# Narrow row loads on GpSimd's own queue, in seven widths, with loads leading stores by six batches

## Chip, cores, metric

One core of one Trainium2 chip. The metric is device time in microseconds of the whole program, median of repeated runs. Ratios below are the mean time of one kernel's fast runs over that of the other's of the same rounds, so not quite the ratio of the medians quoted.

## The reference

A softmax over rows of 256 floats of which only the first `length` count; the rest of the output is zero. There are 16 batches of 2048 rows and one length for a batch, drawn between 128 and 255.

```python
for b in range(batch):
    length = lengths[b]
    masked = x[b, :, :, :length].copy()
    masked = masked - np.max(masked, axis=-1, keepdims=True)
    exp_masked = np.exp(masked)
    result[b, :, :, :length] = exp_masked / np.sum(exp_masked, axis=-1, keepdims=True)
```

The draw is fixed; the prediction lists it. A row is 1024 bytes; columns past the length need not be read.

## The kernel before

A batch sits in SBUF, the core's on-chip memory, as 128 partitions of 16 rows (16 KB to a partition), in one of 12 slots. VectorE clips the columns past the length to a huge negative number, ScalarE takes exponentials and row sums, VectorE scales by the reciprocal sums, and SyncE stores the batch whole. All loads and stores of x go through SyncE's queue, the list of transfers issued by SyncE that the core's 16 DMA engines work off. For each batch SyncE reads the length and loads 160 (or 168), 208 or all 256 columns:

```python
    slots = min(12, batch)
    behind = 2
    widths = [[160, 208], [168, 208]]
    # ...
        def part(b, h, w):
            s = slice(h * half, (h + 1) * half)
            nc.sync.dma_start(
                out=xt[:, b % slots, s, :w], in_=x_f[b, :, s, :w]
            ).then_inc(s_ld[b], 16)
    # ... narrow(b, w): both halves by part; whole(b): one transfer of 2.1 MB
        def load(b):
            pick(length(SP, b), widths[b % 2], lambda w: narrow(b, w), lambda: whole(b))
    # ... batch 0: first half whole, second half by length
        for b in range(1, slots):
            nc.sync.wait_ge(s_fill, b + 1)
            load(b)
        for b in range(batch):
            nc.sync.wait_ge(s_out, b + 1)
            nc.sync.dma_start(out=out_f[b], in_=xt[:, b % slots]).then_inc(s_st[b], 16)
            n = b + slots - behind
            if b >= behind and n >= slots and n < batch:
                nc.sync.wait_ge(s_st[n - slots], 16)
                load(n)
    # ... GpSimd zeroes columns 160 to 255 of all 12 slots first (s_fill; of slot 0 only the second half)
```

A load of whole partitions is one run of 16 KB for each partition; a narrow load is 2048 runs of 640 to 832 bytes, since the columns that are skipped lie between them.

The softmax here doesn't subtract the row's maximum and nothing guards it: scores larger than these inputs give would overflow.

## Time and profile before

| | before |
|---|---|
| time | 162.62 us (162.17 to 162.66, 4 runs) |
| span of the profile | 161.5 us |
| SyncE's queue, share of 16 engines' span | 98.7% |
| VectorE, ScalarE, GpSimd busy | 131.6, 105.2, 15.9 us |
| read and written | 30.28 and 33.55 MB |

The row to look at is the third: the DMA engines are busy all the time and the compute engines are not. "Share" counts the time of packets in flight over 16 engines. The lines are in the prediction.

### The profile page before, as it was taken

To read this page: it belongs to the slowest core of one execution; us is meant where nothing else is said; L and a number is where in the kernel's file an instruction comes from. 1 tells how busy PE (TensorE), PEld (TensorE's weight loads), DVE (VectorE), ACT (ScalarE), POOL (GpSimd) and SP (SyncE) were. 2 spreads that over 40 slices of the span, in tenths; PEclk is the share of its full clock that TensorE was granted. 3 is DMA by queue.
4 is the path that set the end of the run, shared out by engine and by line. 5 is a ranking of instruction groups with operands and counts; after the bars stand their busy time and mean duration, and the time that the engine had idled before them with its cause. 6 is when DMAs were issued, how large, how long until landed. Compare 5 with 4: busy or idle time off the path is not lost.

```text
span 161.5 us, 1141 instructions
## 1 busy us (share of the span) xinstructions
PE 0.2 (0%) x1; PEld 0.1 (0%) x1; DVE 131.6 (82%) x99; ACT 105.2 (65%) x514; POOL 15.9 (10%) x18
## 2 busy tenths in 40 slices
PE   0000000000000000000000000000000000000000
PEld 0000000000000000000000000000000000000000
DVE  4999878999999999999999999999999999000000
ACT  3000089999989797987979797978979892000000
POOL 8999100000000000000000000000000000000000
DMA  5999999999999999999999999999999999999980
GB/s 134 406 414 442 422 378 406 390 356 449 418 376 403 392 290 436 426 430 387 408 405 392 437 430 410 434 422 432 434 422 438 430 430 434 434 426 434 430 357 20
DMA packets 17269, 63.86 MB, mean 396 GB/s; under 512 B 626, under 2 KB 13938, under 8 KB 13938
## 3 DMA queue, kind: packets, MB, share of 16 engines
q1 hardware_dynamic: 17264, 63.83, 98.7%
q14 instruction: 3, 0.02, 0.0%
q10 hardware_dynamic: 2, 0.00, 0.0%
HBM read 30.28 MB, written 33.55 MB: 395 GB/s over the span
## 4 chain that ended last, share of the span: by engine, by line
DVE 65%; issue 15%; ACT 3%; DVEq 1%; POOL 1%; ACTq 0%; PE 0%; POOLq 0%; SPq 0%
DVE xt L206 29%; DVE xt L179 21%; DVE iota_h L154 9%; DVE cap L164 3%; ACT xt L222 3%; DVE inv_sum L204 2%; DVEq L192 1%; POOL xt L132 0%; ACTq L222 0%; POOL iota_i L134 0%; DVEq L191 0%; DVEq L82 0%; DVE len_s L158 0%; PE len_f L143 0%; POOL ones L133 0%
## 5 line engine op out<-in xcount | busy, mean ns | idle before, releaser
L222 ACT ACTIVATE xt<-xt x256 | 102.4, 403 | 27.6 <-DVE xt L179 27.6
L206 DVE TENSOR_TENSOR xt<-xt,inv_sum 128x2048 f32<-128x2048 f32 x32 | 73.4, 2292 | 1.1
L222 ACT ACTIVATION_READ_ACCUMULATOR xt<-xt x256 | 48.3, 188 | 0.0
L179 DVE TENSOR_TENSOR xt<-xt,cap 128x2048 f32<-128x2048 f32 x16 | 36.5, 2283 | 0.3 <-DVE cap L164 0.3
L154 DVE TENSOR_SCALAR iota_h<-iota_i 128x256 f32<-128x256 int32 x1 | 14.6, 14629 | 2.2 <-POOL iota_i L134 2.2
L138 POOL MEMSET xt<- 128x1536 f32 x11 | 14.6, 1367 | 0.0
L204 DVE RECIPROCAL inv_sum<-row_sum 128x8 f32<-128x8 f32 x32 | 6.3, 195 | 1.7 <-ACT xt L222 1.7
L164 DVE TENSOR_SCALAR cap<-iota_h,len_s 128x256 f32<-128x256 f32 x16 | 5.5, 346 | 0.0
L215 ACT ACT_TABLE_LOAD x1 | 1.3, 1283 | 1.5 <-SPq L63 1.5
L132 POOL MEMSET xt<- 128x768 f32 x1 | 0.7, 737 | 0.5 <-SPq L63 0.5
L158 DVE COPY len_s<-len_f 128x16 f32<-128x16 f32 x1 | 0.2, 173 | 0.3 <-PE len_f L143 0.3
L134 POOL IOTA iota_i<- 128x256 int32 x1 | 0.3, 331 | 0.0
L215 ACT ACTIVATE warm<-const-float32-0.0 128x1 f32<-128x1 f32 x1 | 0.2, 203 | 0.0
L133 POOL MEMSET ones<- 1x128 bf16 x1 | 0.2, 194 | 0.0
L143 PE MATMUL len_f<-len_b,ones 1*128 1x16 bf16 x1 | 0.2, 164 | 17.1 <-DVE len_b L156 17.1
L156 DVE CAST len_b<-word 1x16 bf16<-1x16 int32 x1 | 0.1, 150 | 0.0
L244 POOL MEMSET const-float32-0.0<- 128x1 f32 x1 | 0.1, 98 | 0.2 <-issue 0.2
L143 PEld LDWEIGHTS len_f<-len_b,ones 1*128 1x128 bf16 x1 | 0.1, 99 | 17.0 <-issue 17.0
L244 POOL MEMSET const-bfloat16-1.0<- 128x1 bf16 x1 | 0.1, 101 | 0.0
L244 POOL MEMSET const-uint8-127<- 128x1 uint8 x1 | 0.1, 101 | 0.0
L244 POOL MEMSET const-float32-1.0<- 128x1 f32 x1 | 0.1, 98 | 0.0
## 6 DMA issues: line engine op xcount, KB each, us to landing
out_dram<-xt SPq DMA_DIRECT2D x16, 2048.0 KB, 24.0
xt<-in_x_dram SPq DMA_DIRECT2D x9, 2048.0 KB
xt<-in_x_dram SPq DMA_DIRECT2D x9, 832.0 KB, 13.2
xt<-in_x_dram SPq DMA_DIRECT2D x2, 672.0 KB, 12.3
xt<-in_x_dram SPq DMA_DIRECT2D x2, 640.0 KB, 11.6
xt<-in_x_dram SPq DMA_DIRECT2D x1, 1024.0 KB, 5.2
word<-in_lengths_dram ACTq DMA_DIRECT2D x1, 0.1 KB
```

Source lines behind the costliest of these rows:

```text
L132: nc.gpsimd.memset(xt[:, 0, half:, low:], 0.0).then_inc(s_fill, 1)
L138: nc.gpsimd.memset(xt[:, b, :, low:], 0.0).then_inc(s_fill, 1)
L143: nc.tensor.matmul(len_f, lhsT=ones, rhs=len_b, start=True, stop=True).then_inc(s_lenf, 1)
L154: step(nc.vector.tensor_scalar(out=iota_h, in0=iota_i, scalar1=0.5, scalar2=None, op0=ALU.add))
L164: nc.vector.tensor_scalar(out=cap[:, b % 4, :], in0=iota_h, scalar1=len_s[:, b : b + 1], scalar2=-1.0e30, op0=ALU.subtract, op1=ALU.mult,)
L179: return nc.vector.tensor_tensor(out=t[:, :, lo:hi], in0=t[:, :, lo:hi], in1=cap[:, b % 4, None, lo:hi].to_broadcast([P, nt, hi - lo]), op ...
L192: with nc.vector.If(v_len < mid):
L204: step(nc.vector.reciprocal(out=inv_sum[:, b, s], in_=row_sum[:, b, s]))
L206: ins = nc.vector.tensor_tensor(out=t[:, s, :], in0=t[:, s, :], in1=inv_sum[:, b, s, None].to_broadcast([P, half, seq_k]), op=ALU.mult,)
L215: nc.scalar.activation(out=warm, in_=nc.const_aps.tensor(0.0, (P, 1), F32), func=EXP)
L222: ins = nc.scalar.activation(out=e, in_=e, func=EXP, accum_out=row_sum[:, bass.ds(i, 1), j],)
L244: nc = _bacc.Bacc("TRN2", target_bir_lowering=False, num_devices=1)
```

## The change

Three things at once. Narrow loads leave SyncE's queue for GpSimd's own; GpSimd, which is nearly idle, can afford a tree of branches over seven widths. SyncE keeps whole loads and stores. And SyncE's loads lead its stores by six batches, where twelve batches were loaded first and later loads led by ten; the first six are now loaded whole before the lengths are known. GpSimd's loads do not follow the stores: those of batches 6, 9 and 11 are issued as soon as the memsets are done.

```diff
-    behind = 2
-    widths = [[160, 208], [168, 208]]
-    low = 160
+    ahead = min(6, batch)
+    widths = [160, 168, 176, 184, 192, 200, 208]
+    low = widths[0]
@@ one transfer for a batch, on the engine given
+        def narrow(engine, b, w):
+            engine.dma_start(
+                out=xt[:, b % slots, :, :w], in_=x_f[b, :, :, :w]
             ).then_inc(s_ld[b], 16)
+        def pick(v, b, ws):
+            if len(ws) == 1:
+                if ws[0] < seq_k:
+                    narrow(nc.gpsimd, b, ws[0])
                 return
+            m = (len(ws) - 1) // 2
+            with nc.gpsimd.If(v <= ws[m]):
+                pick(v, b, ws[: m + 1])
+            with nc.gpsimd.Else():
+                pick(v, b, ws[m + 1 :])
+        narrow(nc.sync, 0, seq_k)
         nc.scalar.dma_start(out=word64, in_=lengths[None, :]).then_inc(s_word, 16)
+        for b in range(1, ahead):
+            narrow(nc.sync, b, seq_k)
@@ in SyncE's loop, after the store of b
+            n = b + ahead
+            if n < batch:
+                if n < slots:
+                    nc.sync.wait_ge(s_fill, n - ahead + 1)
+                else:
+                    nc.sync.wait_ge(s_st[n - slots], 16)
+                v = length(SP, n)
+                with nc.sync.If(v > widths[-1]):
+                    narrow(nc.sync, n, seq_k)
@@ GpSimd: memsets for slots 6 to 11 only, then its own loads
+        nc.gpsimd.wait_ge(s_word, 16)
+        for n in range(ahead, batch):
+            if n < slots:
+                nc.gpsimd.wait_ge(s_fill, n - ahead + 1)
+            else:
+                nc.gpsimd.wait_ge(s_st[n - slots], 16)
+            v = length(POOL, n)
+            pick(v, n, widths + [seq_k])
@@ VectorE
-            nc.vector.wait_ge(s_ld[b], 32)
+            nc.vector.wait_ge(s_ld[b], 16)
```

More of the change, by code (lines that the diff above doesn't have):

```diff
@@ L17 @@
 ACT = mybir.EngineType.Activation
+POOL = mybir.EngineType.Pool
 @with_exitstack
@@ L86, in length @@
             )
-        def part(b, h, w):
-            s = slice(h * half, (h + 1) * half)
-            nc.sync.dma_start(
-                out=xt[:, b % slots, s, :w], in_=x_f[b, :, s, :w]
+        def narrow(engine, b, w):
+            engine.dma_start(
+                out=xt[:, b % slots, :, :w], in_=x_f[b, :, :, :w]
             ).then_inc(s_ld[b], 16)
-        def narrow(b, w):
-            for h in range(2):
-                part(b, h, w)
-        def whole(b):
-            nc.sync.dma_start(out=xt[:, b % slots], in_=x_f[b]).then_inc(s_ld[b], 32)
-        def pick(v, ws, short, full):
-            if not ws:
-                full()
-                return
-            with nc.sync.If(v <= ws[0]):
-                short(ws[0])
-            with nc.sync.Else():
-                pick(v, ws[1:], short, full)
-        def load(b):
-            pick(length(SP, b), widths[b % 2], lambda w: narrow(b, w), lambda: whole(b))
-        part(0, 0, seq_k)
+        def pick(v, b, ws):
+            if len(ws) == 1:
+                if ws[0] < seq_k:
+                    narrow(nc.gpsimd, b, ws[0])
+                return
+            m = (len(ws) - 1) // 2
[4 more added lines that the diff above has]
+        narrow(nc.sync, 0, seq_k)
         nc.scalar.dma_start(out=word64, in_=lengths[None, :]).then_inc(s_word, 16)
+        for b in range(1, ahead):
+            narrow(nc.sync, b, seq_k)
         nc.sync.wait_ge(s_word, 16)
-        nc.sync.wait_ge(s_fill, 1)
-        pick(length(SP, 0), widths[0], lambda w: part(0, 1, w), lambda: part(0, 1, seq_k))
-        for b in range(1, slots):
-            nc.sync.wait_ge(s_fill, b + 1)
-            load(b)
         for b in range(batch):
@@ L124 @@
             nc.sync.dma_start(out=out_f[b], in_=xt[:, b % slots]).then_inc(s_st[b], 16)
-            n = b + slots - behind
-            if b >= behind and n >= slots and n < batch:
-                nc.sync.wait_ge(s_st[n - slots], 16)
-                load(n)
+            n = b + ahead
[7 more added lines that the diff above has]
+                    narrow(nc.sync, n, seq_k)
         nc.sync.wait_ge(s_st[-1], 16 * slots)
-        nc.gpsimd.memset(xt[:, 0, half:, low:], 0.0).then_inc(s_fill, 1)
         nc.gpsimd.memset(ones, 1.0).then_inc(s_ones, 1)
@@ L136 @@
         ).then_inc(s_iota, 1)
-        for b in range(1, slots):
+        for b in range(ahead, slots):
             nc.gpsimd.memset(xt[:, b, :, low:], 0.0).then_inc(s_fill, 1)
+        nc.gpsimd.wait_ge(s_word, 16)
[6 more added lines that the diff above has]
+            pick(v, n, widths + [seq_k])
         nc.tensor.wait_ge(s_ones, 1)
```

## The prediction

> **What bounds the kernel now.** I read the page's engine and DMA lines first, then the waits of SyncE's queue, then the DMA views of stretches in which only one kind of row moves.
>
> ```profile
> PE 0.2 (0%) x1; PEld 0.1 (0%) x1; DVE 131.6 (82%) x99; ACT 105.2 (65%) x514; POOL 15.9 (10%) x18
> ...
> DMA  5999999999999999999999999999999999999980
> ...
> q1 hardware_dynamic: 17264, 63.83, 98.7%
> ...
> HBM read 30.28 MB, written 33.55 MB: 395 GB/s over the span
> ```
> One DMA queue, SyncE's, keeps the 16 DMA engines busy for 98.7% of the span, from the second slice to the last but one. No compute engine comes near.
>
> ```profile
> SPq L124 <- DVE xt L206: 49.1, 11, 7.0
> SPq L123 <- DMA out_dram<-xt: 22.5, 1, 22.5
> ```
> SyncE's wait for stores at the end lasts 22.5 us, after the last compute: a backlog of stores is drained. The chain of waits names VectorE for 65% of the span, because it follows semaphores and a queue's backlog is not one; I set it aside. VectorE needs about 7.35 us a batch (from one batch's long operations to the next in the chain), against two transfers of nearly 4.9 us for the DMA. So only two things move the end: the work given to the DMA engines, and gaps in which they have none.
>
> Four stretches of the view by windows, the first three with 832-, 672- and 640-byte rows, the last with whole transfers (its last two columns are DMA share and GB/s):
>
> ```profile
> 48.00:51.00 3.00, 0.00 (x0) 0.00 (x0) 2.97 (x3) 3.00 (x17) 0.00 (x0) 1.00 1.13 360
> 57.50:60.50 3.00, 0.00 (x0) 0.00 (x0) 3.00 (x3) 3.00 (x16) 0.00 (x0) 1.00 1.14 287
> 76.60:79.10 2.50, 0.00 (x0) 0.00 (x0) 2.47 (x3) 2.50 (x13) 0.00 (x0) 1.00 1.16 375
> 110.00:140.00 30.00, 0.00 (x0) 0.00 (x0) 27.03 (x22) 22.06 (x110) 0.00 (x0) 1.00 1.01 431
> ...
> DMA packets 1298, 0.86 MB, mean 287 GB/s; under 512 B 16, under 2 KB 1298, under 8 KB 1298
> ...
> DMA packets 1413, 0.94 MB, mean 375 GB/s; under 512 B 21, under 2 KB 1410, under 8 KB 1410
> ```
> In the third, 1410 less 21 completion writes makes 1389 rows in 2.5 us, 356 GB/s; three 16 KB packets raise the 375. The first, in finer slices, stands at 355 until its last. Per row and engine (16 engines x bytes / rate): 640 B cost 28.8 ns, 672 B 37.5, 832 B 37.5. At the whole-row rate (26.9 B/ns an engine) they would cost 23.8, 25.0 and 30.9. The overhead is 5.0, 12.5 and 6.6 ns; 672 is an odd multiple of 32 bytes, the others are even ones. A batch of 2048 rows gives each engine 128, so a load takes 3.68 us (640 B), 4.80 (672 B), 4.80 (832 B), and a whole one, 2.097 MB at 431 GB/s, 4.87. A narrow row saves bytes and almost no time.
>
> **What the Trainium skill says.** "DMA: Bandwidth & Descriptors", section "Why small descriptors are slow (HBM only)", gives a fixed overhead of about 3 cycles a packet, which packing several descriptors into one packet amortizes. The direction agrees; this trace's 5 to 12.5 ns is more. Its section "SWDGE vs HWDGE vs iDMA" says that transfers issued from GpSimd have descriptors made by software, written to rings in SBUF, in packets of preferably at most 4096 B. "Queues, rings and completion order" says that each engine goes round robin over its queues, changing only between packets. With one busy queue the trace shows neither. "SBUF — State Buffer", section "SBUF: two separate sides", says that VectorE's two-port modes and GpSimd exclude each other for a whole instruction. This agrees:
>
> ```profile
> L154 DVE TENSOR_SCALAR iota_h<-iota_i 128x256 f32<-128x256 int32 x1 | 14.6, 14629 | 2.2 <-POOL iota_i L134 2.2
> L138 POOL MEMSET xt<- 128x1536 f32 x11 | 14.6, 1367 | 0.0
> L164 DVE TENSOR_SCALAR cap<-iota_h,len_s 128x256 f32<-128x256 f32 x16 | 5.5, 346 | 0.0
> ```
> A conversion of 256 columns takes 14.6 us, as long as the eleven memsets beside it; operations of that size otherwise take 0.35 us.
>
> **The change part by part.** The lengths are fixed: 188 233 229 243 195 252 165 210 222 180 209 157 159 199 214 248.
>
> Bytes. Before: nine whole loads and the half of batch 0; 832 B for the other half and batches 4, 6, 9, 13; 672 B for batch 11; 640 B for batch 12. After: batches 0 to 5 whole without a test, 7, 8, 10, 14, 15 whole too; batch 6 gets 672 B, 9 gets 736, 11 and 12 get 640, 13 gets 800. That is 30.21 MB against 30.28. The seven widths pay back what the six untested loads give away; bytes gain nothing.
>
> DMA time at the rates above. Before: 16 stores x 4.87 = 77.9; 9.5 whole loads 46.3; 4.5 of 832 B 21.6; one of 672 B 4.8; one of 640 B 3.7; sum 154.3 us. The other 7.2 us of the 161.5 us span are the start, the landing of the last store and small losses. After: stores 77.9; eleven whole loads 53.6; 672 B 4.8; two of 640 B 7.4; 736 and 800 B have no measured row. With 672's overhead (odd multiples of 32 as well) they cost 39.9 and 42.2 ns, 5.1 and 5.4 us; with 6 ns, 4.3 and 4.6. Sum 152.6 to 154.2 us: minus 1.7 to minus 0.1. So with unchanged overheads almost nothing happens.
>
> Packing. If GpSimd's descriptors go six (640, 672 B) or five (736, 800 B) to a packet, most overhead is shared. With 1 to 4 ns left on a row, the five loads have rows of 24.8-27.8 (twice), 26-29, 28.4-31.4 and 30.7-33.7 ns: 128 x 135 to 150 ns = 17.2 to 19.2 us, where the unpacked ones took 21.1 to 22.7. That takes 2 to 5.5 us from the sum.
>
> Start. Five fewer large memsets and none of the half: six x 1.37 = 8.2 us, so the conversion ends near 10 instead of 16.9 and the first mask starts near 11.5 instead of 18.4. The first store can be issued near 23 us (11.5 us from first mask to first result, as before). It gains nothing by itself: six whole loads keep the queue full to 3 + 6 x 4.87 = 32 us, and the narrow loads of 6, 9 and 11 are added from about 12 us.
>
> GpSimd's work: five software transfers and some 50 branches, beside everything. Its descriptor writing may hold up VectorE's 0.35 us operations, perhaps 10 us each time in the worst case; VectorE has 9.7 - 7.35 = 2.4 us of slack a batch and has begun 7 us earlier. Hidden, unless writing takes much longer.
>
> Lead of six. When load n lands, stores and loads of about four batches stand behind it, 39 us, while its own result needs under 15. No gap, provided the narrow load lands in turn.
>
> **The rivals.** (1) Neutral: the overhead of a row belongs to the engine, not the packet. For: the busy share exceeds 1 by only 0.13 in narrow stretches, so rows are handled nearly one after another. Time: 161 to 163 us. (2) Packing: 157 to 160 us. For: what the skill says of GpSimd's packets. Against: no trace of this kernel shows a GpSimd transfer. (3) Starving: each turn passes one row against a 16 KB packet (16384 B at 26.9 B/ns = 0.61 us). Then a narrow load needs 128 x 0.64 = 82 us beside a full queue. Batch 6 then arrives when SyncE's queue runs dry: six loads, stores 0 to 4 and loads 7, 8, 10 are 14 x 4.87 = 68 us, so with some narrow rows between at about 78 us. VectorE masks b+1 before it scales b, so eleven results remain, 11 x 7.35 = 81 us, and a last store of 7 us: 166 to 168 us. With packets of five or six rows a narrow load takes 22 to 26 turns of 0.61 + 0.16 us, about 20 us; batch 6 lands near 40 us, the others follow at 20 us each, all ahead of need. (4) A GpSimd row costs more, since engines must fetch descriptors from SBUF: 5 ns on 640 rows an engine is plus 3.2 us, 165.
>
> **Range and chances.** I hold packing the likeliest, at the weak end of its gain: the overhead is mostly shared, with something lost on switching queues. From 162.6 us, about 3.6 off: 159.0 us. Faster by over 2% (below 159.3): 0.43. Within 2%: 0.34, rival 1 or half of packing. Slower: 0.23, starving or dearer rows. The range is 155 (all overhead gone, VectorE never late) to 168 (starving).
>
> **What would show it.** A stretch with narrow rows beside whole ones moves over 400 GB/s if rows are packed, not 290 to 360. A new software queue carries about 10240 rows, 7.1 MB. The conversion lasts some 8 us instead of 14.6. SyncE's last wait is still long (over 10 us) if the queue never runs dry; if starving, VectorE has an idle gap of ten us or more at batch 6, before 80 us, DMA share falls after it, and that last wait shrinks to one store's time. If VectorE's short operations grow to many us later on, the lock was underrated. I am wrong if a narrow row costs as much on GpSimd's queue as on SyncE's.

## The result

| | before | changed |
|---|---|---|
| time | 162.62 us | 160.40 us (160.11 to 160.63, 4 runs) |
| span of the profile | 161.5 us | 158.5 us |
| SyncE's queue, share | 98.7% | 86.0% |
| GpSimd's queue, share | none | 11.4% |
| read | 30.28 MB | 30.21 MB |

The ratio is 0.9869 (95% interval 0.9843 to 0.9894): 1.3% faster, within 2%. The prediction's figure was 159.0, and the result lies in its range of 155 to 168; but "faster by over 2%" was its likeliest class and did not come. The page of the changed kernel:

```profile
PE 0.2 (0%) x1; PEld 0.1 (0%) x1; DVE 125.6 (79%) x99; ACT 105.1 (66%) x514; POOL 14.5 (9%) x17
...
q1 hardware_dynamic: 3888, 56.62, 86.0%
q0 software_dynamic: 1696, 7.14, 11.4%
...
HBM read 30.21 MB, written 33.55 MB: 402 GB/s over the span
...
L181 DVE TENSOR_TENSOR xt<-xt,cap 128x2048 f32<-128x2048 f32 x16 | 36.6, 2287 | 12.4 <-DMA xt<-in_x_dram 12.0
L91 POOL DMA_DIRECT2D xt<-in_x_dram x5 | 5.9, 1175 | 41.5 <-issue 41.5
L156 DVE TENSOR_SCALAR iota_h<-iota_i 128x256 f32<-128x256 int32 x1 | 8.0, 8030 | 1.6 <-POOL iota_i L128 1.6
```

The queue lines give packets, MB and share. A packet is the piece that an engine moves before it turns to another queue; a completion write is a packet of 4 bytes, 16 to a transfer. GpSimd's queue moved the 10240 rows of its five loads in only 1696 packets, of which 80 are completion writes: a packet holds six or seven rows (4416 to 4800 bytes in the packet records). It took 11.4% of 158.5 us, 18.1 us of every engine for five loads; whole loads would take 24.4. The DMA is nearly as full as before: 97.5% of the span together, against 98.7%. The waits of SyncE's queue:

```profile
SPq L114 <- DVE xt L208: 107.2, 15, 12.3
SPq L113 <- DVE xt L208: 18.6, 1, 18.6
SPq L113 <- DMA out_dram<-xt: 14.3, 1, 14.3
```

The last line says that 14.3 us of stores are still queued when nothing else is left. So the 12.0 us for which VectorE stood waiting for loads cost nothing: the DMA never ran dry.

The gain therefore lies in DMA time, and so does what is missing from it. This is a stretch of the DMA view with batch 6's 672-byte rows on one queue and the whole loads of batches 2 and 3 on the other (no store is issued before 22.7 us, and the first stands behind them):

```profile
DMA packets 468, 4.67 MB, mean 389 GB/s; under 512 B 16, under 2 KB 16, under 8 KB 250
## 3 DMA queue, kind: packets, MB, share of 16 engines
q1 hardware_dynamic: 234, 3.57, 78.2%
q0 software_dynamic: 234, 1.10, 23.0%
```

It covers 12 us. The queues pass packet for packet, 234 to 234. A packet of GpSimd's is 1.10 MB / 234 = 4704 bytes, seven rows. Of SyncE's 234, 16 are completion writes; the 218 of 16 KB took 78.2% of 16 x 12 us, 689 ns each, where 16 KB at the whole-row rate take 610. GpSimd's took 23.0%, 189 ns, where 4704 bytes would take 175. A turn, one packet of each queue, thus carries 79 + 14 = 93 ns too much, 13 ns for each of seven rows. That is what such a row cost on SyncE's queue (12.5 ns in the kernel before). The overhead is not gone, only charged mostly to the packet next to it.

### The profile page after: what moved, and what is told of

It reads as the page before. It is cut to its first block, busy times and chain, and to the rows that moved or that the text cites. A ratio compares the mean times of both kernels' runs of the same rounds, so it can differ in the third digit from the quotient of the medians.

```text
span 158.5 us, 1141 instructions
## 1 busy us (share of the span) xinstructions
PE 0.2 (0%) x1; PEld 0.1 (0%) x1; DVE 125.6 (79%) x99; ACT 105.1 (66%) x514; POOL 14.5 (9%) x17
## 3 DMA queue, kind: packets, MB, share of 16 engines
q0 software_dynamic: 1696, 7.14, 11.4%
HBM read 30.21 MB, written 33.55 MB: 402 GB/s over the span
## 4 chain that ended last, share of the span: by engine, by line
DVE 48%; DMA 26%; issue 11%; ACT 3%; DVEq 0%; SPq 0%; POOL 0%; ACTq 0%; PE 0%; POOLq 0%
DMA xt<-in_x_dram 26%; DVE xt L208 23%; DVE xt L181 15%; DVE iota_h L156 5%; ACT xt L224 3%; DVE cap L166 2%; DVE inv_sum L206 2%; DVEq L194 0%; ACTq L224 0%; POOL iota_i L128 0%; SPq L114 0%; SPq L83 0%; DVEq L193 0%; DVE len_s L160 0%; PE len_f L145 0%
## 5 line engine op out<-in xcount | busy, mean ns | idle before, releaser
L224 ACT ACTIVATION_READ_ACCUMULATOR xt<-xt x256 | 47.8, 187 | 0.0
L91 POOL DMA_DIRECT2D xt<-in_x_dram x5 | 5.9, 1175 | 41.5 <-issue 41.5
L156 DVE TENSOR_SCALAR iota_h<-iota_i 128x256 f32<-128x256 int32 x1 | 8.0, 8030 | 1.6 <-POOL iota_i L128 1.6
L132 POOL MEMSET xt<- 128x1536 f32 x6 | 8.0, 1367 | 0.0
## 6 DMA issues: line engine op xcount, KB each, us to landing
xt<-in_x_dram POOLq DMA_DIRECT2D x2, 1280.0 KB, 38.7
xt<-in_x_dram POOLq DMA_DIRECT2D x1, 1344.0 KB, 20.8
```

The lines of the kernel that those rows point to most:

```text
L91: engine.dma_start(out=xt[:, b % slots, :, :w], in_=x_f[b, :, :, :w]).then_inc(s_ld[b], 16)
L132: nc.gpsimd.memset(xt[:, b, :, low:], 0.0).then_inc(s_fill, 1)
L156: step(nc.vector.tensor_scalar(out=iota_h, in0=iota_i, scalar1=0.5, scalar2=None, op0=ALU.add))
L224: ins = nc.scalar.activation(out=e, in_=e, func=EXP, accum_out=row_sum[:, bass.ds(i, 1), j],)
```

## The experiments

Two theories. **A**: the overhead of a narrow row stays in the engine's work on the SBUF side, whatever packet the row is in; GpSimd's queue hides it only where the packet in turn with it is a store. **B**, the prediction's: packing shares it, and switching between queues costs back a part. A further rival, **C**: the earlier start and the lead made the gain. Three jobs, each with its own runs of the kernel before, on one chip each. "Packed rows alone", "A second queue" and "Stores only" were run once, for their traces; the state of a single run is unknown, and no conclusion rests on their times.

**The queue undone.** SyncE issues the narrow loads itself, with the same widths and the same lead; batches 6, 9 and 11 are now issued after a store, as the others.

```diff
-                if ws[0] < seq_k:
-                    narrow(nc.gpsimd, b, ws[0])
+                narrow(nc.sync, b, ws[0])
@@ and nc.sync.If / nc.sync.Else in pick
-                with nc.sync.If(v > widths[-1]):
-                    narrow(nc.sync, n, seq_k)
+                pick(v, n, widths + [seq_k])
@@ GpSimd's loop of loads removed
```

> The changed kernel with its narrow loads put back on SyncE's queue; same widths, same order, same lead of six. Theory A (the overhead of a narrow row stays in the engine's writing to SBUF; on GpSimd's queue it is hidden only while a store is the other packet in turn) and rival B (packets of six or seven rows on GpSimd's queue share the overhead, and a fixed cost of switching between queues takes back a part) both say that the queue is the gain: the sum for row-by-row transfers, 152.6 to 154.2 us plus 7.2 us, 161.5 to 163.5 us in time. Rival C (the gain comes from the earlier start and the lead of six, not from the queue): 160.4 us as the changed kernel.

161.99 us (161.79 to 162.45), ratio 0.9961 (0.9943 to 0.9979). The changed kernel, in its three jobs, has 0.9869, 0.9857 and 0.9849. So of the 1.4%, the queue makes about 1.0%, 1.7 us, and widths, order and start together 0.4%, 0.6 us. C is wrong as the main cause. The run also issues batch 6's load 13 us later, but that is not what cost the time: the gate below delays it by 26 us on GpSimd's queue and loses nothing.

**No narrow loads.**

```diff
-                v = length(SP, n)
-                with nc.sync.If(v > widths[-1]):
-                    narrow(nc.sync, n, seq_k)
+                narrow(nc.sync, n, seq_k)
@@ GpSimd's loop of loads removed
```

> The changed kernel with every load whole and none on GpSimd's queue: 67.1 MB in 32 transfers of 4.87 us. The packet records of the changed kernel give its five narrow loads 17.8 us and the 16 KB packets beside them about 3.2 us more than before, 21.0 us in all, against 24.4 us for five whole loads. A and B: plus 3.4 us, 163.8 us. C (neither the narrow rows nor their queue matter): 160.4 to 161 us.

165.58 us (165.07 to 165.82), ratio 1.0177 (1.0155 to 1.0198). Narrow rows are worth more than I expected, some 5 us beside GpSimd's queue and 3.6 on SyncE's.

```profile
span 163.6 us, 1075 instructions
...
q1 hardware_dynamic: 4608, 67.11, 96.9%
```

The span grew by 5.1 us. Busy share times span is 158.5 us here and 154.5 (97.5% of 158.5) in the changed kernel, 4.0 us of the 5.1; the other 1.1 us is time in which engines stood idle. 0.8 us of it lies in the last 10 us of the span (DMA share 0.58, against 0.66 in the changed kernel); why the engines run out less evenly there was not tested. The run also gives the measure for a full queue: 158.5 / 32 = 4.95 us a transfer. At that rate the changed kernel's 27 whole transfers should take 133.7 us; they took 86.0% of 158.5, 136.3. The 2.6 us between are, by this estimate, the rows' overhead that landed in 16 KB packets.

**Even widths.** I suspected odd multiples of 32 bytes.

```diff
-    widths = [160, 168, 176, 184, 192, 200, 208]
+    widths = [160, 176, 192, 208]
```

> Widths 160, 176, 192, 208 only: rows are even multiples of 32 bytes; batches 6, 9 and 13 carry 8 columns more, 0.2 MB or 0.46 us. A: the dear rows (odd multiples of 32 bytes, 12.5 ns each on SyncE's queue against 5 to 6.6) become cheaper where they run beside loads, 0.8 us for batch 6 and 0.3 for batch 9, so 159.4 to 160.0 us, and the stretch with batch 6's rows rises from 389 to over 400 GB/s. B: width parity does not matter, only bytes: 160.9 us, and that stretch stays near 389 GB/s.

160.22 us (159.82 to 160.56), ratio 0.9842 (0.9821 to 0.9863): the same as the changed kernel's within the intervals. Batch 6's rows are now 704 bytes; the stretch from 14 to 26 us moves 393 GB/s, against 389, and the two repeats of the unedited kernel moved 393 there as well:

```profile
14.00:26.00 12.00, 0.00 (x0) 0.00 (x0) 10.61 (x9) 12.00 (x62) 0.00 (x0) 1.00 1.00 393
```

So parity was the wrong idea, in the prediction and here. The run with the queue undone shows it more directly. Its DMA view has 736-byte rows alone from 68.5 to 70.5 us and 800-byte rows alone from 104.5 to 106.5:

```profile
DMA packets 858, 0.63 MB, mean 316 GB/s; under 512 B 0, under 2 KB 858, under 8 KB 858
DMA packets 916, 0.74 MB, mean 370 GB/s; under 512 B 0, under 2 KB 915, under 8 KB 915
```

858 and 915 rows in 2 us on 16 engines are 37.3 and 35.0 ns a row. 800 is an odd multiple of 32 bytes, yet its overhead of 5.3 ns (35.0 less 29.7) is below the 6.6 of 832, an even one. A simpler reading fits: with the 37.5 ns of 672 and of 832 bytes (kernel before), a row between 672 and 832 bytes costs 35 to 38 ns whatever its width. Only 640 is clearly cheaper. Why there is a step I did not test.

**Packed rows alone.**

```diff
+        for b in (6, 9, 11):
+            nc.sync.wait_ge(s_ld[b], 16)
         narrow(nc.sync, 0, seq_k)
```

> SyncE holds its loads back until batches 6, 9 and 11 have landed from GpSimd's queue, so that packed narrow rows run with nothing beside them; the total is of no interest (some 15 us longer). A: the rates of SyncE's queue come back although the rows are packed: about 287 GB/s for 672-byte rows and 356 for 640-byte rows. B: packing has removed the overhead: about 400 GB/s for both.

173.21 us, as little to the point as expected. Two stretches by windows, with 672-byte and with 640-byte rows (last two columns: DMA share, GB/s), in which no other engine works:

```profile
13.00:16.50 3.50, 0.00 (x0) 0.00 (x0) 0.00 (x0) 0.00 (x0) 0.00 (x0) 1.00 1.03 304
22.20:24.40 2.20, 0.00 (x0) 0.00 (x0) 0.00 (x0) 0.00 (x0) 0.00 (x0) 1.00 1.02 360
```

The DMA view of the same two stretches, and between them of batch 9's 736-byte rows from 17.5 to 21 us:

```profile
q0 software_dynamic: 234, 1.06, 102.8%
...
DMA packets 249, 1.10 MB, mean 314 GB/s; under 512 B 0, under 2 KB 0, under 8 KB 249
...
q0 software_dynamic: 178, 0.79, 101.7%
```

GpSimd's queue alone, packets of 4.5 KB (1.06 MB / 234, 0.79 MB / 178), and the rates are 304, 314 and 360 GB/s for 672, 736 and 640 bytes. Row by row on SyncE's queue they were 287, 316 and 356; B wanted 400. This settles it against B: a packet of six or seven rows saves nearly nothing by itself. That packing does save and a dearer row on GpSimd's queue takes it back, by the same amount at three widths, is not excluded; the run shows only the two together.

**The changed kernel again**, for comparison with the next two.

> The changed kernel itself, unedited, on the chip of the next two, so that they have it beside them: 160.4 us.

160.24 us (159.94 to 160.89), ratio 0.9857 (0.9834 to 0.9881).

**Only the queue, in the old order.** The kernel before, with the narrow halves of batches 1 to 15 issued by GpSimd after its eleven memsets.

```diff
-        def part(b, h, w):
+        def part(b, h, w, engine=nc.sync):
@@ narrow(b, w): part(b, h, w, nc.gpsimd)
-            pick(length(SP, b), widths[b % 2], lambda w: narrow(b, w), lambda: whole(b))
+            with nc.sync.If(length(SP, b) > widths[b % 2][-1]):
+                whole(b)
@@ GpSimd: for b in 1..15, wait for the memset (or the slot's store), then narrow by its length
```

> The kernel before, its order of loads (twelve batches first, then stores) and its widths untouched, with only the narrow loads of batches 1 to 15 moved to GpSimd's queue. Batches 4, 6, 9 and 11 (832 and 672 bytes) then run beside whole loads alone, 12 and 13 beside stores. A (the overhead is hidden only beside a store): only 12 and 13 gain, about 1.2 us from 162.7, so 161.2 to 162.2 us. B (packing or merely a second queue hides it): 832 bytes 4.8 to 4.1 us four times, 672 bytes 4.8 to 3.5, 640 bytes 3.7 to 3.3, together 4.5 us off, 158 us.

169.06 us (168.70 to 169.13), ratio 1.0381 (1.0365 to 1.0398): 6.3 us slower than before. Both expectations missed. The DMA's busy tenths by slices and GpSimd's 832-byte issues, from the page (the last number is us to landing):

```profile
DMA  5999999999999999999999999999999934774993
...
xt<-in_x_dram POOLq DMA_DIRECT2D x8, 832.0 KB, 46.8
```

And VectorE's wait, from the waits:

```profile
DVE xt L196 <- DMA xt<-in_x_dram: 20.9, 3, 11.7
```

Here the DMA does run dry, from the 33rd slice (134 us) on. The cause is the turns. An 832-byte half takes 13 packets an engine, a 672- or 640-byte half 10; twelve halves make 144 turns. With a 16 KB packet between each two, a turn lasts about 0.8 us (0.61 + 0.17), so GpSimd's queue needs some 115 us for them, an estimate from the packet times of this trace; its packet records have the first at 21.0 us and the last completion at 131.5. Batches 12 and 13 come last in it and come too late. The queue alone is a loss. In the changed kernel it is a gain, with 101 turns instead of 144 and the lead of six; which of these is needed was not tested, so the three quarters above hold for taking the queue away, not for adding it alone.

**A gate**, to let batch 6's rows meet stores.

```diff
         nc.gpsimd.wait_ge(s_word, 16)
+        nc.gpsimd.wait_ge(s_ld[ahead - 1], 16)
```

> The changed kernel, with GpSimd waiting until batch 5 has landed before its first narrow load, so that batch 6's 672-byte rows and batch 9's 736-byte ones meet mostly stores. A: the 16 KB packets beside them fall from about 690 and 670 ns to under 640, 18 turns by 70 ns and 11 by 55 an engine, less what later rows now meet loads: 1.0 to 1.8 us off, 158.8 to 159.5 us, and the first stretch of batch 6's rows moves over 410 GB/s, not 389. B (a fixed cost of switching queues): no change, 160.4. A rival to both: the narrow loads now land too late for VectorE, and the time rises above 161.

159.89 us (159.33 to 160.20), ratio 0.9821 (0.9800 to 0.9843), against 0.9857 for the changed kernel beside it: 0.35 us less by the medians, and the intervals overlap. A miss for A's size. The reason is in a stretch of 4 us from 44 us on:

```profile
q1 hardware_dynamic: 75, 1.23, 80.2%
q0 software_dynamic: 70, 0.33, 21.3%
```

80.2% of 16 x 4 us over 75 packets is 684 ns: by the order of its transfers, SyncE's queue had by then reached the load of batch 7, and batch 6 met a load after all. SyncE's last wait for stores shrank from 14.0 us (changed kernel, same job) to 8.4, so lateness used up slack too.

**A second queue without packets of several rows.** ScalarE issues batch 6's load on its hardware queue.

```diff
+        nc.scalar.wait_ge(s_word, 16)
+        nc.scalar.wait_ge(s_fill, 1)
+        v6 = length(ACT, ahead)
+        with nc.scalar.If(v6 <= 168):
+            narrow(nc.scalar, ahead, 168)
@@ else 208; GpSimd starts with batch 7
```

> Batch 6's narrow load, and only that, issued before its loop by ScalarE on a hardware queue of its own, so that it is a second queue without packets of several rows. If turns go by packet (the prediction's third rival, starving): one 672-byte row a turn against 16 KB, some 18 GB/s for it while SyncE's queue is full, batch 6 lands when that queue runs dry or after 128 turns of 0.65 us (80 to 95 us after issue), VectorE idles over ten us before batch 6, and the time is 166 to 172 us. If a second queue simply shares the engines' time: it lands within 25 us of its issue and the time stays at 160 to 161 us.

181.52 us, and the starving is there as described. The DMA view from 14 to 26 us (q10 is ScalarE's queue):

```profile
q1 hardware_dynamic: 268, 3.90, 81.4%
q0 software_dynamic: 170, 0.75, 15.7%
q10 hardware_dynamic: 271, 0.18, 4.8%
```

VectorE's wait, and the issue on the page:

```profile
DVE xt L181 <- DMA xt<-in_x_dram: 43.2, 2, 41.9
```

```profile
xt<-in_x_dram ACTq DMA_DIRECT2D x1, 1344.0 KB, 90.3
```

3.90 MB are 238 packets of 16 KB, beside 271 of a single row: about one row a turn, 15 GB/s, and 90.3 us to landing. With seven rows a packet the same batch needed 20.8. So the packets do matter, for the turns rather than for the overhead. The time overshot the expected 172 because batch 6 landed at 94 us of the span, where the prediction's sum had 78: eleven results at 7.35 us and a last store of 7 from there make 182, near the 179.7 us of the span.

**Stores only**, by holding SyncE back.

```diff
+                if n == ahead + 1:
+                    nc.sync.wait_ge(s_ld[ahead], 16)
@@ and the gate above
```

> GpSimd waits until batch 5 has landed, and SyncE holds batch 7's load back until batch 6 has landed, so that for some 10 us batch 6's 672-byte rows meet stores and nothing else. A: there the 16 KB packets take 611 to 620 ns, not 690, and the stretch moves about 420 GB/s, where the same rows beside loads moved 389 and alone 287. If the overhead belongs to the switch between queues: 389 GB/s as beside loads. The total is of no interest.

162.15 us, and no answer to its question: the first packet of the rows moved at 41.2 us, 5.5 us after GpSimd began to issue them, when SyncE's two stores were nearly done, so the rows ran alone again. The windows view shows 324 GB/s from 43 to 45 us and 278 from 45 to 47, about the packed-alone result. The next run answers instead.

**Loads behind loads.** If A is right, loads should stand in one queue and stores in the other.

```diff
-                if ws[0] < seq_k:
+                if ws[0] < seq_k or b < slots + 2:
                     narrow(nc.gpsimd, b, ws[0])
@@ SyncE
-            if n < batch:
-                if n < slots:
-                    nc.sync.wait_ge(s_fill, n - ahead + 1)
-                else:
-                    nc.sync.wait_ge(s_st[n - slots], 16)
+            if slots + 2 <= n < batch:
+                nc.sync.wait_ge(s_st[n - slots], 16)
```

> A version meant to be faster: the whole loads of batches 7, 8 and 10 go through GpSimd's queue too, in order with the narrow ones; SyncE keeps stores and the loads of 14 and 15. Narrow rows from batch 9 on then meet stores, not loads; batch 6's still meet loads 1 to 5. A: about 1 us less than the changed kernel beside it, 158.8 to 159.6 us. If the overhead is one of switching queues, there are more switches and no gain: 160.2 us or above. If whole loads in GpSimd's queue delay the narrow ones behind them too long, over 161 us, with VectorE waiting for batch 12 or 13.

> The changed kernel, unedited, beside the one before this on the same chip: 160.2 to 160.4 us.

159.33 us (159.14 to 159.59), ratio 0.9779 (0.9760 to 0.9799), against 160.27 (160.11 to 160.98), ratio 0.9849 (0.9824 to 0.9875), for the changed kernel: 0.9 us less, as expected of A, with a correct output, and the fastest of all kernels here. Loads and stores also stand in another order, but the gain lies in the packets: the queues' shares on the page

```profile
q1 hardware_dynamic: 3456, 50.33, 76.5%
q0 software_dynamic: 2128, 13.44, 20.8%
```

are together 97.3% of 157.4 us, 153.2 us of busy engines, against 97.6% of 158.4, 154.6 us, beside it. The stretch from 51 to 61 us, where batch 9's 736-byte rows meet stores alone:

```profile
DMA packets 461, 4.26 MB, mean 426 GB/s; under 512 B 32, under 2 KB 32, under 8 KB 263
## 3 DMA queue, kind: packets, MB, share of 16 engines
q1 hardware_dynamic: 229, 3.23, 76.7%
q0 software_dynamic: 231, 1.02, 25.7%
```

3.23 MB are 197 packets of 16 KB at 76.7% of 16 x 10 us, 623 ns each; GpSimd's 231 packets of 4416 bytes, six rows, took 178 ns, where 164 are data. Too much by 13 + 14 ns a turn, 4.5 ns a row; the same rows cost 9.9 ns too much row by row (37.3 less 27.4). The queues take turns at least as fast as before (231 in 10 us, 234 in 12) and the rate is near the 431 GB/s of whole transfers. It is not the switching that costs.

The changed kernel's own packet records say the same. SyncE's 16 KB packets were counted off in order of start, 128 to a transfer, which tells loads from stores. Their median was 671 ns in a load and 619 in a store beside batch 9's 736-byte rows, 634 and 616 beside batch 11's 640-byte rows, 649 and 614 beside batch 13's 800-byte rows, and 611 in loads and in stores that no rows meet.

## Why the prediction was right or wrong

**What bounds it: right.** The DMA engines are full in both kernels, and SyncE's wait at the end is long in both (22.5 and 14.3 us).

**The range: no proof.** 155 to 168 us held all four rivals, so a result inside it favours none, and 160.40 lies in the gap between packing (157 to 160) and neutral (161 to 163).

**Bytes gain nothing, and unchanged overheads change little: right.** Rival 1's 161 to 163 us is what the undone queue measured, 161.99. Its reason, that the overhead belongs to the engine and not to the packet, is what the packed rows alone support; that stores hide it was in no rival. The guess by parity was wrong: an 800-byte row costs 35.0 ns, where it gave 42.2.

**Packing: right that several rows go in a packet (six or seven; five or six were expected) and that the five loads take 17.2 to 19.2 us on their queue (18.1 measured); wrong that this is all they cost.** The step that failed is "most overhead is shared", with "1 to 4 ns left on a row". The prediction's own sign, "I am wrong if a narrow row costs as much on GpSimd's queue as on SyncE's", came true for rows that run alone. The sentence of the Trainium skill that it cites for packing limits it to small descriptors (see the last section), and the prediction left that half out. Of the five loads, 16.6 us are data (7.14 MB at 26.9 B/ns an engine). With the 18.1 us and the 2.6 us found in the 16 KB packets beside them, the overhead is 4.1 us, 6.4 ns for each of 640 rows an engine: 13 for batch 6's rows beside loads, near 4.5 for batch 9's beside stores. The gain expected was 3.6 us, the gain measured 2.2. The signal named beforehand, "over 400 GB/s if rows are packed, not 290 to 360", came out between, 389 beside loads, and 426 beside stores.

**Start: right in size.** The conversion took 8.03 us, the first mask started at 11.13 us, the first store was issued at 22.74. Its worth was not measured by itself; with widths and order it is the 0.6 us above.

**GpSimd's work: too careful.** Issuing a transfer kept GpSimd 1.18 us, not up to 10, and VectorE's 0.35 us operations rose from a mean of 346 to 359 ns.

**Lead of six: half right.** "All ahead of need" is wrong: the narrow loads queue behind each other, took a median of 38.7 us to land in the width used twice, and VectorE waited 12.0 us for data. "No gap" for the DMA is right, and only that counted.

**Starving: rightly kept as a rival, and shown.** It needs packets of one row. The run on ScalarE's queue landed batch 6 after 90.3 us (82 predicted for 128 turns).

**Dearer rows on GpSimd's queue: wrong** in sum, 304, 314 and 360 GB/s alone against 287, 316 and 356.

Shown by runs: taking the queue away loses three quarters of the gain; packing alone saves nearly nothing; loads with loads and stores with stores is better. Argued only: that the hidden part is work on the SBUF side. A store's neighbour hides it and a load's does not, which fits, but no run separates writing SBUF from reading HBM. The step between 640 and 672 bytes is unexplained, as is the 1.1 us of idle DMA time in the run of whole loads.

## What to carry to other kernels

When many short rows must be loaded, look at what is in turn with them on the other queues: here a stretch of loads beside loads kept the rows' overhead, and loads beside stores hid most of it. A second queue is served packet for packet, so count its turns against the other queue's packet size before moving work there, and check that its last item still lands in time. Shorter rows are not faster in proportion: measure the cost of a row at each width first.

## What the Trainium skill lacked or had wrong

- "DMA: Bandwidth & Descriptors", section "Why small descriptors are slow (HBM only)": it says that packing consecutive descriptors amortizes the fixed cost of a packet and is only worth it for descriptors of at most 256 bytes. The runs agree with both halves taken together: for rows of 640, 672 and 736 bytes it saved hardly anything, 360, 304 and 314 GB/s packed and alone, against 356, 287 and 316 row by row. What it lacks is that the cost can be hidden beside transfers in the other direction (16 KB packets of 623 ns beside rows and stores, 689 beside rows and loads).
- The same page, "SWDGE vs HWDGE vs iDMA": packets of at most 4096 bytes "preferably". Here they are 4704 (seven rows of 672) and 4416 bytes (six of 736).
- The same page, "Anatomy of one DMA — SWDGE (gpsimd) path": it calls the time of descriptor generation small and variable. What it lacks is a figure by rows: a load of 2048 rows kept GpSimd 1.18 us, and its first packet moved 2.0 us after the issue began in the run of packed rows alone, 4.6 us after it in the changed kernel.
- The same page, "Queues, rings and completion order": the round robin by packet agrees (234 packets to 234). It lacks that on a hardware queue each row is a packet of its own, so that such a queue gets about one 672-byte row a turn (271 rows beside 238 packets of 16 KB, 90.3 us to landing).
- "SBUF — State Buffer", section "SBUF: two separate sides": it says that the loser of the shared ports waits for a whole instruction. It lacks that the wait can last a whole run of them: the conversion took 8.03 us beside six memsets of 1.37 us and 14.63 beside eleven.
- No page gives a measured time of a row by its width: 28.8 ns at 640 bytes, 37.5 at 672, 37.3 at 736, 35.0 at 800, 37.5 at 832.
